# Sums over the partitions in a two-layer trunk: one fp32 matmul with ones against two fp32r matmuls on a split

## The chip, the core and the metric

The kernel runs on one core of a Trainium2 chip. The core has TensorE (PE in the profile, its weight loads PEld), VectorE (DVE), ScalarE (ACT), GpSimd (POOL) and SyncE (SP, which here issues the DMAs). Each engine takes its instructions in the order of its own queue and waits on semaphores for the others. The metric is device time in microseconds (us) of one execution, the median of several.

## The reference

The program is a decoder trunk of two layers on x of 1024 tokens by 1024 channels, in float32. In each layer the input is normalised, projected, and handed to four token mixers (latent attention "a", a gated convolution "b", a pooling "c", sliding-window attention "d"); their outputs are normalised per group, projected back and added; then comes a gated FFN of width 2816, normalised and added too. A last normalisation ends it. Every normalisation is this one:

```python
def rmsnorm(x, g):
    xf = x.astype(jnp.float32)
    y = xf * lax.rsqrt(jnp.mean(xf * xf, axis=-1, keepdims=True) + RMS_EPS)
    return (y * g.astype(jnp.float32)).astype(x.dtype)
...
for l in range(DEPTH):
    h = rmsnorm(x, attn_norm[l])
    proj = h @ w_in[l]
    ...
    q = (rmsnorm(c_q, q_norm_g) @ w_uq)
    kv = (rmsnorm(c_kv, kv_norm_g) @ w_ukv)
    ...
    gf = gf * lax.rsqrt(jnp.mean(gf * gf, axis=-1, keepdims=True) + RMS_EPS)   # per mixer
    x = x + mixed @ w_o[l]
    h2 = rmsnorm(x, ffn_norm[l])
    x = x + (jax.nn.silu(gate) * up) @ w_down[l]
return rmsnorm(x, final_norm)
```

## The kernel before

Activations lie with the channel on the partitions and the token along the row, so a tile is 128 channels by 512 tokens; the 1024 tokens are two halves t = 0 and 1. A sum over channels is therefore a sum over the partitions.

**Matrix products in three parts.** Products are made in the type fp32r. To keep more of the fp32 digits, each fp32 operand is split in two: `split` (L278 to L286) has ACT copy the tile into an fp32r tile `hi` (L280, or L283 with a gain) and DVE subtract that from the original into `lo` (L281 or L284). `mm3` (L264 to L276, its matmul is L269) then makes hi·hi, hi·lo and lo·hi into one PSUM bank. Nearly all of TensorE's instructions are of this line. In the FFN combinations of operands replace some of the products (lines named by B11 to T4), which does not touch the change.

**The norm.** `SumSq` holds the sum of squares of one normalisation, an accumulator `acc[t]` for each half. `add` squares a tile on ACT into a buffer of tag "tn" (L315; the first tile is squared straight into the accumulator, L310) and adds it on DVE (L321; the last addition also adds the epsilon, L317; L312 where there is one tile only). `rnorm` makes the reciprocal root: a matmul with a 128x128 tile of ones sums over the partitions and gives every partition the total (L327), ACT takes logarithm, exponential and square (L329, L330, L331), and one Newton step on DVE mends the digits (L332, L335), the last back into the accumulator. Callers then multiply by it (mostly through `mul_to`, L339).

`rnorm` is called 35 times: twice at the start (L364), in each layer twice for each of the four mixers' outputs (L608 for c, d and b, L1026 for a), twice for the key and value latents (L747), twice for the query latents (L788), twice ahead of the FFN (L1415), and at the end of a layer for the next norm (L1629 to L1641). In the last layer the second half is made in two pieces of 256 columns, so that gives three calls there.

**Buffers.** Most tiles live in 47 places of 128x1024 that `Slots` hands out. Scratch tiles come from `tmp`, with three tags: "te" has two buffers, "tn" three, "tp" three. "tn" is used by `add`, by `rnorm` (two a call), by the attention mixers' last steps (L575, L967) and by `snap` in the FFN. PSUM's eight banks have the tags "mm" (2), "s" (3), "t" (2) and "pv" (1); `rnorm` takes "t", before and after the FFN "pv", and for the last pieces "s". A buffer is used again once the instructions that read it have finished.

**Order.** The kernel is written for a tile framework: it places the waits, and when the program is built it lays each engine's instructions in an order that need not be that of the text. All DMAs of the main loop are issued by SP.

Of the kernel before, what the change touches and what calls it, by code (L numbers as in the profile page):

```python
# [11 lines left out]
F32 = mybir.dt.float32  # L12
F32R = mybir.dt.float32r
# [4 lines left out]
P = 128  # L18
# [3 lines left out]
HT = 512  # L22
# [88 lines left out]
def trunk_kernel(ctx: ExitStack, tc: tile.TileContext, ins, out):  # L111
    nc = tc.nc
    act, dve, pe, pool, sp = nc.scalar, nc.vector, nc.tensor, nc.gpsimd, nc.sync

    cpool = ctx.enter_context(tc.tile_pool(name="const", bufs=1))
    wpool = ctx.enter_context(tc.tile_pool(name="w", bufs=2))
    tpool = ctx.enter_context(tc.tile_pool(name="tmp", bufs=6))
# [7 lines left out]
    def rd(ap):  # L125
        return ap.bitcast(F32)
# [3 lines left out]
    pool.dma_start(par, ins["params"])  # L130
    cst = cpool.tile([P, CC_N], F32, name="cst")
    ident = cst[:, CC_ID : CC_ID + P]
    ones = cpool.tile([P, P], F32, name="ones")
    dve.memset(ones, 1.0)
    e_r = cpool.tile([P, P], F32R, name="e_r")
    nsink = cpool.tile([P, L * 4], F32, name="nsink")
    nffn = cpool.tile([P, L * NK], F32, name="nffn")
# [36 lines left out]
    def ps(tag):  # L174
        if tag in turns:
            turns[tag].rotate(-1)
            tag = turns[tag][-1]
        return psum.tile([P, HT], F32, name=f"ps_{tag}", tag=tag, bufs=PS_BUFS[tag])

    def tmp(tag="te"):  # L180
        return tpool.tile([P, HT], F32, name=tag, tag=tag, bufs={"te": 2, "tn": 3, "tp": 3}[tag])

    def small(n):
        return spool.tile([P, n], F32, name=f"sm{n}", tag=f"sm{n}", bufs=16 if n < 16 else 2)
# [93 lines left out]
    def split(hi, lo, f, gain=None):  # L278
        if gain is None:
            act.copy(hi, f)  # L280
            dve.tensor_tensor(out=lo, in0=f, in1=rd(hi), op=ALU.subtract)  # L281
        else:
            act.activation(hi, f, AF.Copy, scale=gain)  # L283
            dve.scalar_tensor_tensor(  # L284
                out=lo, in0=f, scalar=gain, in1=rd(hi), op0=ALU.mult, op1=ALU.subtract
            )  # L286
# [8 lines left out]
    class SumSq:  # L295
# [7 lines left out]
        def add(self, t, f, cols=whole):  # L303
            e = EPS * self.n / P
            m = self.done[t, cols.start] = self.done.get((t, cols.start), 0) + 1
            if self.acc[t] is None:
                self.acc[t] = F.half()
            a = F.ap(self.acc[t])[:, cols]
            if m == 1:
                act.activation(a, f, AF.Square)  # L310
                if self.n == P:
                    dve.tensor_scalar(out=a, in0=a, scalar1=e, scalar2=None, op0=ALU.add)  # L312
                return
            q = tmp("tn")[:, cols]
            act.activation(q, f, AF.Square)  # L315
            if m == self.n // P:
                dve.scalar_tensor_tensor(  # L317
                    out=a, in0=q, scalar=e, in1=a, op0=ALU.add, op1=ALU.add
                )
            else:  # L320
                dve.tensor_tensor(out=a, in0=a, in1=q, op=ALU.add)  # L321

        def rnorm(self, t, cols=whole, tag="t"):

            a, n = F.ap(self.acc[t])[:, cols], self.n
            p = ps(tag)[:, cols]
            pe.matmul(p, ones, a, start=True, stop=True)  # L327
            r0, q = tmp("tn")[:, cols], tmp("tn")[:, cols]
            act.activation(r0, p, AF.Ln, scale=1.0 / n)  # L329
            act.activation(r0, r0, AF.Exp, scale=-0.5)  # L330
            act.activation(q, r0, AF.Square)  # L331
            dve.scalar_tensor_tensor(  # L332
                out=q, in0=p, scalar=-0.5 / n, in1=q, op0=ALU.mult, op1=ALU.mult
            )
            dve.scalar_tensor_tensor(out=a, in0=q, scalar=1.5, in1=r0, op0=ALU.add, op1=ALU.mult)  # L335
            return self.acc[t]
# [41 lines left out]
    for l in range(L):  # L378
# [38 lines left out]
        def swa_q(m, pp):  # L417
            for t in range(2):
                f = tmp()
                dve.scalar_tensor_tensor(  # L420
                    out=f, in0=pp[t], scalar=0.125, in1=r_of(t), op0=ALU.mult, op1=ALU.mult
                )
                e, o = R.half(), R.half()
                qs[2 * m][t], qs[2 * m + 1][t] = e, o
                act.copy(R.ap(e)[hd], f[hd])
                act.copy(R.ap(o)[tl], f[tl])
                dve.tensor_tensor(
                    out=R.ap(e)[tl], in0=f[hd], in1=rd(R.ap(e)[hd]), op=ALU.subtract
                )
                dve.tensor_tensor(  # L430
                    out=R.ap(o)[hd], in0=f[tl], in1=rd(R.ap(o)[tl]), op=ALU.subtract
                )
# [40 lines left out]
        for t in range(2):  # L473
            f = tmp()
            mul_to(f, pv_[t], r_of(t))
            p = ps("t")
# [196 lines left out]
        for ct in range(2):  # L673
            pp = nextp
            u, a, b = F.pair(), F.pair(), F.pair()
# [36 lines left out]
            for t in range(2):  # L712
                h, lo = half_split(dst[:, t * HT : (t + 1) * HT])
                p = ps("t")
# [42 lines left out]
        for t in range(2):  # L757
            p = ps("mm")
            for k in range(NK):
                for n in range(2):  # L760
# [4 lines left out]
                        start=k == 0 and n == 0,  # L765
                        stop=k == NK - 1 and n == 1,
# [9 lines left out]
            p = ps("t")  # L776
# [804 lines left out]
        for n, (c, m) in enumerate(units):  # L1581
# [19 lines left out]
            p = banks["c" if c in (B21, N1, B22) else "a", m]  # L1601
# [169 lines left out]
```

## Time and profile before

| what | value |
|---|---|
| median of 3 runs | 2095.85 us (2094.59 to 2098.07) |
| span of the profiled execution | 2092.6 us |
| PE, DVE, ACT, POOL busy | 2057.8, 1493.1, 977.7, 539.8 us |
| matmuls of L327 | 70 (66 of 512 columns, 4 of 256) |
| granted TensorE clock | 0.998 of full speed |
| mean DMA rate | 138 GB/s |

The span runs from the first to the last instruction of the profiled execution; about 3 us lie around it in a run's time. In rows of groups the columns are line, engine, operation, output and inputs by name, shapes and count, then busy time and mean ns of one, then the idle time of the engine just before them with what ended it. In rows of the timeline they are start, duration, engine, line, operation, names, shapes and count, and in brackets the idle time before. Matmuls are pipelined: one that follows another shows a duration longer than the distance between their starts. In rows of windows the columns are the stretch, its length, and the busy time with the number of instructions of PE, PEld, DVE, ACT and POOL. In rows of the chain of waits they are start, duration and what the chain runs through.

### The profile page before, as it was taken

The page shows a single profiled execution, that of the slowest core. Times are in us where ns is not written, and L with a number is a line of the kernel's source. Part 1 is how long each engine was busy: PE and PEld are TensorE (multiplying, and loading weights), DVE is VectorE, ACT ScalarE, POOL GpSimd, SP SyncE. Part 2 cuts the span into 40 slices and gives each one's busy share as a digit, 9 for nine tenths or more (in the row PEclk, how much of TensorE's full clock was granted, in tenths as well). Part 3 has the DMA queues.
Part 4 walks back from the last instruction along what each step waited for, and adds up shares of the span by engine and source line. Part 5 has one row for each costly group of instructions (what it writes and reads, how often), then busy time and mean ns, then how long its engine had stood idle before and what let it go on. Part 6 is the DMA issues. An engine that isn't in the chain of part 4 may idle for free.

```text
span 2092.6 us, 26301 instructions
## 1 busy us (share of the span) xinstructions
PE 2057.8 (98%) x9442; PEld 1679.2 (80%) x9442; DVE 1493.1 (71%) x2407; ACT 977.7 (47%) x1706; POOL 539.8 (26%) x453
## 2 busy tenths in 40 slices
PE   8999999999999999999999999999999999999997
PEld 6777787888888888888888777877878888888887
DVE  6878977877666767566656889869666676675655
ACT  6446656653333334454433566657423333344442
POOL 0000000037676674200000000000467667541000
PEclk9999999999999999999999999999999999999999
DMA  4010122424444446886401102232354444378752
GB/s 178 33 51 26 68 87 73 161 72 169 172 156 151 166 161 201 290 289 220 147 28 51 46 13 92 68 117 100 112 180 161 143 174 156 126 259 312 260 178 88
DMA packets 148819, 289.76 MB, mean 138 GB/s; under 512 B 12608, under 2 KB 72000, under 8 KB 148688
## 3 DMA queue, kind: packets, MB, share of 16 engines
q1 hardware_dynamic: 148656, 288.03, 39.8%
q8 instruction: 74, 1.21, 0.2%
q14 instruction: 57, 0.47, 0.1%
q0 software_dynamic: 32, 0.04, 0.0%
HBM read 204.66 MB, written 83.36 MB: 138 GB/s over the span
## 4 chain that ended last, share of the span: by engine, by line
PE 92%; DVE 4%; ACT 2%; DMA 1%; issue 1%; POOL 0%; DVEq 0%; ACTq 0%; SPq 0%; POOLq 0%
PE ps_mm L269 35%; PE ps_s L269 28%; PE ps_t L269 12%; PE ps_pv L269 8%; PE ps_pv L953 2%; PE ps_t L941 1%; PE ps_t L327 1%; PE ps_s L887 1%; PE ps_pv L563 1%; PE ps_s L888 1%; PE ps_t L551 1%; PE ps_s L889 1%; PE ps_s L502 0%; DMA u<-in_w_o 0%; DVE u L281 0%
## 5 line engine op out<-in xcount | busy, mean ns | idle before, releaser
L269 PE MATMUL ps_mm<-u,u 128*128 128x512 f32 (+1 forms) x3376 | 825.2, 391 | 10.6 <-ACT u L283 6.9
L269 PEld LDWEIGHTS ps_mm<-u,u 128*128 128x128 f32 x3376 | 616.8, 189 | 132.9 <-ACT u L283 6.9
L269 PE MATMUL ps_s<-u,u 128*128 128x512 f32 x2672 | 630.8, 390 | 3.5 <-ACT tn L1167 3.5
L269 PEld LDWEIGHTS ps_s<-u,u 128*128 128x128 f32 x2672 | 501.5, 188 | 110.4 <-ACT tn L1167 4.3
L281 DVE TENSOR_TENSOR u<-u,u 128x1024 fp32r<-128x1024 f32 (+2 forms) x368 | 423.6, 1167 | 175.5 <-ACT u L280 155.3
L280 ACT CAST u<-u 128x1024 fp32r<-128x1024 f32 (+2 forms) x368 | 321.4, 897 | 485.1 <-PE ps_mm L269 182.3
L269 PE MATMUL ps_t<-u,u 128*128 128x512 f32 (+1 forms) x1212 | 274.5, 379 | 0.0
L269 PEld LDWEIGHTS ps_t<-u,u 128*128 128x128 f32 x1212 | 219.1, 188 | 44.1 <-issue 1.4
L950 POOL MEMSET u<- 128x128 f32 x32 | 6.4, 225 | 870.5 <-PE ps_mm L269 653.5
L158 POOL TENSOR_TENSOR u<-u 128x256 f32<-128x256 f32 x176 | 187.0, 1063 | 92.6 <-DMA u<-in_w_dn 62.7
L1303 POOL TENSOR_TENSOR tp<-tp,u 128x512 f32<-128x512 f32 x88 | 127.0, 1444 | 291.2 <-ACT tp L1302 290.9
L269 PE MATMUL ps_pv<-u,u 128*128 128x512 f32 x696 | 164.9, 389 | 0.0
L269 PEld LDWEIGHTS ps_pv<-u,u 128*128 128x128 f32 x696 | 130.7, 188 | 27.1
L1302 ACT ACTIVATE tp<-tp 128x512 f32<-128x512 f32 x88 | 55.5, 632 | 123.0 <-DVE tp L339 122.1
L280 ACT CAST u<-ps_t 128x512 fp32r<-128x512 f32 (+4 forms) x136 | 66.3, 505 | 67.4 <-PE ps_t L941 42.8
L281 DVE TENSOR_TENSOR u<-ps_t,u 128x512 fp32r<-128x512 f32 (+4 forms) x136 | 77.5, 582 | 25.7 <-ACT u L280 24.8
L283 ACT ACTIVATE u<-u,par 128x512 fp32r<-128x512 f32 x100 | 69.4, 715 | 51.2 <-DVE u L1090 16.5
L1123 POOL TENSOR_TENSOR u<-u,u 128x512 f32<-128x512 f32 x38 | 65.6, 1727 | 85.5 <-PE ps_s L269 44.5
L284 DVE SCALAR_TENSOR_TENSOR u<-u,par,u 128x512 fp32r<-128x512 f32 x100 | 72.8, 745 | 9.4 <-ACT u L283 9.1
L1515 DVE TENSOR_TENSOR tp<-ps_mm,tn 128x512 f32<-128x512 f32 x38 | 26.3, 692 | 68.7 <-PE ps_mm L269 68.7
L213 DVE TENSOR_TENSOR u<-u,u 128x1024 fp32r<-128x1024 f32 (+1 forms) x46 | 51.7, 1128 | 29.0 <-PE ps_t L269 10.0
L1296 DVE SCALAR_TENSOR_TENSOR u<-te,tp 128x512 f32<-128x512 f32 x38 | 44.9, 1182 | 36.8 <-POOL tp L1303 36.8
(188 smaller groups left out, 2248.7 us busy)
## 6 DMA issues: line engine op xcount, KB each, us to landing
u<-in_w_gu SPq DMA_DIRECT2D x88, 512.0 KB, 4.0
ad<-u SPq DMA_DIRECT2D x154, 256.0 KB, 2.2
u<-ad SPq DMA_DIRECT2D x70, 512.0 KB, 5.4
u<-in_w_dn SPq DMA_DIRECT2D x68, 512.0 KB, 3.8
qd<-u SPq DMA_DIRECT2D x44, 512.0 KB, 2.9
u<-qd SPq DMA_DIRECT2D x32, 512.0 KB, 5.2
u<-in_w_in SPq DMA_DIRECT2D x30, 512.0 KB, 3.5
u<-in_xT SPq DMA_DIRECT2D x32, 256.0 KB, 4.5
```

The lines of the kernel that those rows point to most:

```text
L158: pool.tensor_tensor(out=o, in0=o, in1=u, op=ALU.add)
L213: dve.tensor_tensor(out=lo[:, :n], in0=raw[:, :n], in1=rd(hi[:, :n]), op=ALU.subtract)
L269: pe.matmul(o, w, r, start=start and k == 0 and i == 0, stop=stop and k == n - 1 and i == 2, skip_group_check=again,)
L280: act.copy(hi, f)
L281: dve.tensor_tensor(out=lo, in0=f, in1=rd(hi), op=ALU.subtract)
L283: act.activation(hi, f, AF.Copy, scale=gain)
L284: dve.scalar_tensor_tensor(out=lo, in0=f, scalar=gain, in1=rd(hi), op0=ALU.mult, op1=ALU.subtract)
L953: pe.matmul(py[:, c0:], v_of(j, h), R.ap(s)[:, c0:], start=j == 0 and n == 0, stop=j == nj - 1 and n == 1,)
L1123: pool.tensor_tensor(out=F.ap(q + 1), in0=a21, in1=a22, op=ALU.add)
L1296: dve.scalar_tensor_tensor(out=o, in0=a, scalar=-1.0, in1=b, op0=ALU.mult, op1=ALU.mult)
L1302: last_silu = act.activation(g, g, AF.Silu)
L1303: pool.tensor_tensor(out=g, in0=g, in1=r, op=ALU.mult)
```

## The change

`rnorm` splits the accumulator into two fp32r tiles of tag "tn", with `split` as the products do, and makes two matmuls with ones, one for each part, into the same bank. The tile of ones is declared fp32r, and `tmp` takes a type. The rest of `rnorm` stays, so a call takes four buffers of "tn" where it took two, and issues one copy on ACT and one subtraction on DVE more.

```diff
-    ones = cpool.tile([P, P], F32, name="ones")
-    dve.memset(ones, 1.0)
+    ones = cpool.tile([P, P], F32R, name="ones")
+    dve.memset(ones.bitcast(F32), 1.0)
...
-    def tmp(tag="te"):
-        return tpool.tile([P, HT], F32, name=tag, tag=tag, bufs={"te": 2, "tn": 3, "tp": 3}[tag])
+    def tmp(tag="te", dt=F32):
+        return tpool.tile([P, HT], dt, name=tag, tag=tag, bufs={"te": 2, "tn": 3, "tp": 3}[tag])
...
             a, n = F.ap(self.acc[t])[:, cols], self.n
             p = ps(tag)[:, cols]
-            pe.matmul(p, ones, a, start=True, stop=True)
+            ah, al = tmp("tn", F32R)[:, cols], tmp("tn", F32R)[:, cols]
+            split(ah, al, a)
+            pe.matmul(p, ones, ah, start=True, stop=False)
+            pe.matmul(p, ones, al, start=False, stop=True)
             r0, q = tmp("tn")[:, cols], tmp("tn")[:, cols]
             act.activation(r0, p, AF.Ln, scale=1.0 / n)
```

## The prediction

> **What bounds the kernel now.** I read the page first: its head, the busy shares and the engine shares of the chain that ended last.
>
> ```profile
> span 2092.6 us, 26301 instructions
> PE 2057.8 (98%) x9442; PEld 1679.2 (80%) x9442; DVE 1493.1 (71%) x2407; ACT 977.7 (47%) x1706; POOL 539.8 (26%) x453
> PE 92%; DVE 4%; ACT 2%; DMA 1%; issue 1%; POOL 0%; DVEq 0%; ACTq 0%; SPq 0%; POOLq 0%
> ```
>
> TensorE sets the end for 92% of the span. Work taken off it there shortens the kernel; the 6% of the chain on DVE and ACT are where added steps of those two lengthen it. The question is on which part each `rnorm` lies. Next the view of line L327, the matmul that is replaced.
>
> ```profile
> L327 PE MATMUL ps_t<-u,ones x52: 590/592/697, 31.8 to 1408.9; 128*128 128x512 f32 x52
> L327 PE MATMUL ps_pv<-u,ones x14: 590/592/697, 415.9 to 2052.1; 128*128 128x512 f32 x14
> L327 PE MATMUL ps_s<-u,ones x4: 379/431/483, 2066.0 to 2082.9; 128*128 128x256 f32 x4
>   DVE u L317: 10.0, 12
> ```
>
> Seventy records make 35 calls: one fp32 matmul runs as two instructions. 33 calls are 512 columns wide, two 256. The last row says that TensorE sat idle before this line 12 times, 10.0 us in all, for L317, the addition that completes the sum of squares; before the other 23 it did not wait for it. Then the windows by engine, over the stretch of each layer where the calls crowd (the last row is the first window for L327 alone: 18 of its matmuls, so 9 calls, and the second has as many), and the time behind the first one.
>
> ```profile
> 180.00:240.00 60.00, 57.84 (x248) 43.45 (x246) 58.00 (x105) 42.91 (x81) 0.34 (x2) 1.00 0.10 34
> 1212.00:1272.00 60.00, 57.87 (x247) 43.36 (x246) 58.04 (x106) 42.73 (x82) 0.35 (x2) 1.00 0.10 33
> 260.00:365.00 105.00, 102.90 (x525) 82.18 (x524) 82.14 (x213) 60.78 (x148) 2.81 (x14) 1.00 0.25 81
> 180.00:240.00 60.00, 9.16 (x18) 2.88 (x18) 1.00 0.10 34
> ```
>
> In these two stretches DVE (third pair of numbers) is busy 58.00 of 60 us, as full as TensorE (first pair, 57.84). Later it has room (82.14 of 105). Last the timeline and the chain, which are quoted where they are used.
>
> **Removed: the fp32 matmul.** The timeline of TensorE around the first call, and a run of fp32r matmuls before it:
>
> ```profile
> 26.61 5.38 PE L269 MATMUL ps_s<-u,u 128*128 128x512 f32 x23
> 31.59 0.40 PE L269 MATMUL ps_s<-u,u 128*128 128x512 f32 x1
> 31.83 0.59 PE L327 MATMUL ps_t<-u,ones 128*128 128x512 f32 x1
> 32.26 0.59 PE L327 MATMUL ps_t<-u,ones 128*128 128x512 f32 x1
> 32.29 0.80 PE L269 MATMUL ps_s<-u,u 128*128 128x512 f32 x1
> ```
>
> The second half starts 0.43 us after the first. The fp32r matmul behind shows 0.80 us and ends at 33.09, where one of the usual 0.40 (second row) would have begun at 32.69, another 0.43 on. So the call holds the array for about 0.86 us. In the run of 23 fp32r matmuls the pitch is (5.38 - 0.40) / 22 = 0.23 us; the two new matmuls are of that form and take 0.46. That is 0.40 us less in each wide call, and half, 0.20, in a narrow one: 33 x 0.40 + 2 x 0.20 = 13.6 us of TensorE. The number of weight loads stays. The Trainium skill, "FP8 and Floating Point Precision", section "TensorE Precision Notes", has true FP32 at four passes; with four passes of the 0.23 us pitch a call would hold 0.92 us and the change would free 33 x 0.46 + 2 x 0.23 = 15.6 us. The row, 0.86, decides here.
>
> **Added: the split.** No call of before has it. The nearest forms are the split of a 128x512 SBUF tile, and for the narrow calls that of a 128x256 one:
>
> ```profile
> L280 ACT CAST u<-te 128x512 fp32r<-128x512 f32 x20 | 12.3, 615 | 3.8 <-DVE te L339 3.7
> L281 DVE TENSOR_TENSOR u<-te,u 128x512 fp32r<-128x512 f32 x20 | 13.7, 685 | 0.1
> L280 ACT CAST u<-vraw 128x256 fp32r<-128x256 f32 x2 | 0.8, 404 | 0.0
> L281 DVE TENSOR_TENSOR u<-vraw,u 128x256 fp32r<-128x256 f32 x2 | 0.8, 408 | 0.0
> 182.41 1.28 DVE L339 TENSOR_TENSOR u<-u,u 128x512 f32<-128x512 f32 x2
> ```
>
> ACT gets 35 copies, 21 us on an engine at 47%. DVE gets 35 subtractions; one shows 0.685 us, but back to back they follow at 1.28 - 0.68 = 0.60 us (last row), so 20.8 us in all. They bring two waits: DVE's subtraction waits for the copy, and everything in DVE's queue behind it waits too (evacuations of PSUM banks among it); the second matmul waits for the subtraction, with TensorE's queue behind it. No DMA is added and SP and POOL get nothing.
>
> What this costs where nothing hides it, read from the chain of waits in the prologue and at the end:
>
> ```profile
> 43.86 0.70 DVE u L317
> 44.61 1.14 PE ps_t L327 x2
> 45.83 0.61 ACT tn L329
> ...
> 48.58 0.70 DVE u L335
> ...
> 2082.09 0.44 DVE u L317
> 2082.57 0.71 PE ps_s L327 x2
> 2083.36 0.39 ACT tn L329
> ```
>
> From the end of L317 to the start of Ln (L329) is 45.83 - 44.56 = 1.27 us now. With the split, and hand-overs of 0.05 to 0.1 as between these rows: 0.1, copy 0.615, 0.05, subtraction 0.685, 0.05, second matmul 0.40, 0.1 = 2.0; so +0.7 us for a wide call on the chain, the saving on TensorE already inside. In the narrow one 0.84 now, and 0.1 + 0.40 + 0.05 + 0.41 + 0.05 + 0.28 + 0.1 = 1.39 then: +0.55. (0.28 is my estimate for a 256-column matmul, 0.40 less half a pitch.)
>
> Three calls stand alone on the chain so: these two, and one at the entry of the second layer's FFN, where TensorE waits for the addition:
>
> ```profile
> 1435.59 1.10 PE L327 MATMUL ps_pv<-u,ones 128*128 128x512 f32 x2 [0.94 <-DVE u L317]
> ```
>
> Together 0.7 + 0.7 + 0.55 = +1.9 us.
>
> **The crowded stretch** is the term I had to choose. The chain enters it through DVE, runs through TensorE, and near its end TensorE waits twice, for ACT and for DVE:
>
> ```profile
> 180.69 0.61 DVE u L317
> 181.43 1.96 PE ps_t L327 x4
> 183.39 2.75 PE ps_mm L761 x12
> ...
> 229.84 1.18 PE ps_s L269 x5
> ```
>
> ```profile
> 232.67 0.50 PE L887 MATMUL ps_s<-u,u 128*128 128x512 f32 x1 [1.04 <-ACT u L280]
> 239.21 1.13 PE L327 MATMUL ps_t<-u,ones 128*128 128x512 f32 x2 [0.92 <-DVE u L317]
> ```
>
> Nine calls give DVE 9 x 0.60 = 5.4 us of new work there, and it has 60 - 58.00 = 2.0 us idle. If DVE sets the pace, the stretch grows by 3.4 us when all its idle time can be used and by 5.4 when none can; TensorE's saving, 9 x 0.40 = 3.6, then only makes its waits longer. If TensorE sets the pace and DVE's backlog is work that nobody needs yet, the stretch shrinks by 3.6. So its growth x lies between -3.6 and +5.4 by these rows. I take the middle of the upper case, +4.4: the stretch ends, at 231 and 239 us, with TensorE waiting for DVE and ACT. It comes twice: +8.8.
>
> **The other calls.** 35 less 18 less 3 are 14, one of them narrow: 13 x 0.40 + 0.20 = 5.4 us saved. They lie where TensorE has other matmuls to run while the split is made and DVE is below 80% (260 to 365 us above). That cover exists because the order on an engine is not that of the text: a weight load of a much later step is issued before the first call.
>
> ```profile
> 27.57 0.77 SPq L209 DMA_DIRECT2D vraw<-in_w_uq  x1
> ```
>
> Without that cover each of the 14 would cost +0.7 instead of -0.4.
>
> **Sum:** 8.8 + 1.9 - 5.4 = +5.3 us on the profiled execution, whose span of 2092.6 is 3.25 below the median 2095.85. I add it to the median: 2101.1 us.
>
> **Rivals.** In all of them the time is 2095.85 + 2x + 1.9 - 5.4, and x decides; it breaks even at x = 1.75.
>
> (a) TensorE keeps the pace, x = -3.6, 2085.2 us: faster. For it: between the rows at 183.39 and 229.84 the chain runs through TensorE alone, and DVE can put off work whose results are needed late. Against it: the two waits above. It counts as faster from x below -0.35. If the three lone calls were covered too, the whole 13.6 would arrive: 2082.3. The Trainium skill, "Perfetto Trace Analysis", section "Identifying the Most-Contended Engine", says to improve the engine with the highest occupancy first, which is TensorE's 98% here; its next section adds that this engine may change between regimes, and the windows show just that.
>
> (b) DVE puts off part of the backlog, x between -0.35 and 3.85, about 2096: no change that could be measured.
>
> (c) Buffers. Tag "tn" has three; a call took two and now takes four, and the additions and snapshots use the tag too. It is tight already:
>
> ```profile
> 186.79 0.68 DVE L335 SCALAR_TENSOR_TENSOR u<-tn 128x512 f32<-128x512 f32 x1
> 187.57 0.63 ACT L331 ACTIVATE tn<-tn 128x512 f32<-128x512 f32 x1
> 207.68 0.68 DVE L335 SCALAR_TENSOR_TENSOR u<-tn 128x512 f32<-128x512 f32 x1
> ```
>
> L331 of one call, which takes a tn buffer, starts only when L335 of the call before has released its own (186.79 + 0.68 = 187.47). From the end of L317 (180.69 + 0.61 = 181.30) the first call takes 6.2 us to that point; alone, in the prologue, a call takes 48.58 + 0.70 - 44.56 = 4.7. If the calls can no longer overlap, the first five (they feed keys and queries) need 5 x (6.2 + 0.7) = 34.5 us; now the last of them ends with the third row, at 208.36, after 27.1. Then x is 7.4 and the time 2095.85 + 14.8 - 3.5 = 2107.1. It decides once the pieces of a later call hold two buffers while an earlier one needs its last.
>
> **Chances.** Less than about 0.2%, 4.2 us, can't be told from no change. Forecast (x over 3.85, DVE) 0.33; buffers 0.15; so slower 0.48. Rival (b) 0.25 same. Rival (a) 0.27 faster. The range runs from almost the full gain, 2083, past the buffers' 2107 to 2113 (the 14 covered calls half uncovered, 7 x 1.1 us, on top of the forecast's 2101 give 2109 too); some 0.15 is left outside it for an order of instructions that turns out quite differently. The forecast's own range is 2100 to 2104 (x from 3.85 to 5.4).
>
> **What would show it.** Right: in the windows of the two stretches DVE at 59 of 60 or more, the last L327 of the stretch later by 3 us or more after the first, and the waits near 232 and 239 us longer, while the other 14 calls start with no wait for L280 or L281. TensorE busy down by some 13 us and its idle time up by more. Rival (a): the same distance shorter, DVE's new work found after 240. Rival (c): Square or the copies waiting for a release of tn by DVE or PE. Wrong at the root: if the two new matmuls follow at more than 0.23 us each, or the copy and the subtraction cost clearly other than 0.62 and 0.60.

## The result and the profile after

The changed kernel takes 2122.43 us (median of 4 runs, 2120.34 to 2124.83) against 2095.68 for the kernel before: a ratio of 1.0131, 95% interval [1.0116, 1.0145], so 26.7 us slower. It is above the range of the forecast. The profiled execution has a span of 2123.1 us, 30.5 longer than the one of before. It is the slowest of the four runs, and differences between the two traces come out some 4 us larger than that of the medians.

The page of the changed kernel, head and busy shares:

```profile
span 2123.1 us, 26375 instructions
PE 2066.3 (97%) x9442; PEld 1685.6 (79%) x9442; DVE 1516.7 (71%) x2442; ACT 995.8 (47%) x1741; POOL 538.6 (25%) x453
```

DVE and ACT have 35 instructions more, as they should. TensorE, which was to lose 13 us of busy time, shows 8.5 more; the last section gives a part of the reason. Below the changed kernel's lines are L328 (the split), L329 and L330 (the two matmuls), L332 (Ln); L317 and the lines above it are those of before. In its timeline, the first call of all and two calls of the first crowded stretch show the parts of the change as they run. (The prediction counted nine calls in a stretch, those in its window of 60 us. A tenth stands just ahead of the window, at 176.26 and 1207.86 us in the kernel before. "First call" here is the first of the nine, the same one in every kernel.)

```profile
32.50 0.40 PE L329 MATMUL ps_t<-tn,ones 128*128 128x512 f32 x1
32.74 0.39 PE L330 MATMUL ps_t<-tn,ones 128*128 128x512 f32 x1
32.97 3.36 PE L269 MATMUL ps_s<-u,u 128*128 128x512 f32 x14
...
183.94 0.39 PE L329 MATMUL ps_t<-tn,ones 128*128 128x512 f32 x1
...
186.26 0.39 PE L330 MATMUL ps_t<-tn,ones 128*128 128x512 f32 x1
...
189.18 0.50 PE L329 MATMUL ps_t<-tn,ones 128*128 128x512 f32 x1
```

The starts lie 0.24 and 0.23 us apart: a call holds the array for 0.47 us, as worked out. But in the stretch the first call's second matmul comes 2.3 us after its first, with other work between, and the second call 5.2 us after the first. In the kernel before both calls ran in one group of four matmuls, at 181.43.

Where the time lies is read from the last call of each crowded stretch in the changed kernel's timeline (the first and the third row below; the second is the first call of the second layer's stretch), and, in a second fence, from the first and last call of the second layer's stretch in the kernel before:

```profile
255.65 0.50 PE L329 MATMUL ps_t<-tn,ones 128*128 128x512 f32 x1
...
1232.25 0.40 PE L329 MATMUL ps_t<-tn,ones 128*128 128x512 f32 x1
...
1301.22 0.50 PE L329 MATMUL ps_t<-tn,ones 128*128 128x512 f32 x1
```

```profile
1213.04 0.67 PE L327 MATMUL ps_t<-u,ones 128*128 128x512 f32 x1 [0.20 <-DVE u L317]
...
1270.76 1.12 PE L327 MATMUL ps_t<-u,ones 128*128 128x512 f32 x2 [0.92 <-DVE u L317]
```

From the first call of a stretch to its last it was 239.21 - 181.43 = 57.78 us in the first layer and 57.72 in the second; now it is 71.71 and 68.97. These two growths, 13.9 and 11.3, are 25.2 of the 30.5 us of span. Now the windows by engine for the changed kernel:

```profile
180.00:240.00 60.00, 52.26 (x193) 38.94 (x193) 50.35 (x83) 39.13 (x69) 0.34 (x2) 0.86 0.05 18
```

DVE was to be full here, 59 of 60. It is busy 50.35, less than before (58.00). Nothing is full: TensorE fell from 57.84 to 52.26, and its granted clock in this stretch to 0.86. The 60 us also hold less of the work than before: 193 of TensorE's matmuls, where there were 248. So the engines wait for each other. What TensorE waited for from 176 to 256 us, the view of waits (total, times, longest), before and then after:

```profile
PE ps_t L327 <- DVE u L317: 1.1, 2, 0.9
PE ps_s L887 <- ACT u L280: 1.0, 1, 1.0
```

```profile
PE ps_t L329 <- ACT tn L280: 4.4, 2, 4.0
PE ps_mm L269 <- DVE u L823: 1.8, 1, 1.8
PE ps_t L781 <- ACT u L280: 1.1, 1, 1.1
PE ps_t L330 <- DVE tn L281: 1.1, 1, 1.1
PE ps_s L890 <- ACT u L280: 1.0, 1, 1.0
PE ps_s L269 <- DVE u L284: 0.5, 1, 0.5
```

2.1 us of waits have become 9.9 in these rows. The wait for the new copy (first row) is the largest, but 3.4 us are new waits for operands that the change doesn't touch (L823, L280 ahead of L781, L284).

### The profile page after: what moved, and what is told of

It is laid out like the page before. It is cut to its first block, busy times and chain, and to the rows that moved or that the text cites. A ratio compares the mean times of both kernels' runs of the same rounds, so it can differ in the third digit from the quotient of the medians.

```text
span 2123.1 us, 26375 instructions
## 1 busy us (share of the span) xinstructions
PE 2066.3 (97%) x9442; PEld 1685.6 (79%) x9442; DVE 1516.7 (71%) x2442; ACT 995.8 (47%) x1741; POOL 538.6 (25%) x453
## 4 chain that ended last, share of the span: by engine, by line
PE 88%; DVE 5%; ACT 3%; DMA 2%; issue 1%; POOL 0%; DVEq 0%; ACTq 0%; SPq 0%; POOLq 0%
PE ps_mm L269 33%; PE ps_s L269 27%; PE ps_t L269 12%; PE ps_pv L269 7%; PE ps_pv L956 2%; PE ps_t L944 1%; PE ps_s L890 1%; ACT u L280 1%; PE ps_pv L566 1%; PE ps_s L892 1%; PE ps_s L891 1%; PE ps_t L554 1%; PE ps_mm L764 1%; DMA u<-in_w_o 1%; DMA u<-in_w_gu 1%
## 5 line engine op out<-in xcount | busy, mean ns | idle before, releaser
L269 PE MATMUL ps_mm<-u,u 128*128 128x512 f32 (+1 forms) x3376 | 834.0, 393 | 11.8 <-ACT u L283 7.1
L280 ACT CAST u<-u 128x1024 fp32r<-128x1024 f32 (+2 forms) x368 | 321.0, 897 | 479.9 <-PE ps_mm L269 179.0
L280 ACT CAST u<-ps_t 128x512 fp32r<-128x512 f32 (+4 forms) x136 | 66.7, 504 | 69.5 <-PE ps_t L944 39.5
L281 DVE TENSOR_TENSOR u<-ps_t,u 128x512 fp32r<-128x512 f32 (+4 forms) x136 | 78.2, 583 | 25.1 <-ACT u L280 23.9
L284 DVE SCALAR_TENSOR_TENSOR u<-u,par,u 128x512 fp32r<-128x512 f32 x100 | 72.1, 747 | 12.1 <-ACT u L283 11.7
```

The costliest lines, as they stand in the source:

```text
L269: pe.matmul(o, w, r, start=start and k == 0 and i == 0, stop=stop and k == n - 1 and i == 2, skip_group_check=again,)
L284: dve.scalar_tensor_tensor(out=lo, in0=f, scalar=gain, in1=rd(hi), op0=ALU.mult, op1=ALU.subtract)
```

## The experiments

Three theories stood against each other at first: work (the copy and the subtraction fill DVE and ACT), waiting (the matmul is held back by the 1.3 us of the split), and buffers (tag tn has three, a call needs four). A fourth came out of the runs.

**Where the loss sits: e6, e7.** The change is made only in the calls outside the two stretches (e6: mixer a, ahead of the FFN, and the 512-column calls at the ends of the layers, 11 in all), or only in the 20 calls of the stretches, ten in each layer (e7).

```diff
-        def rnorm(self, t, cols=whole, tag="t"):
+        def rnorm(self, t, cols=whole, tag="t", parts=False):
...
+            if parts:
+                ah, al = tmp("tn", F32R)[:, cols], tmp("tn", F32R)[:, cols]
+                split(ah, al, a)
+                pe.matmul(p, ones_r, ah, start=True, stop=False)
+                pe.matmul(p, ones_r, al, start=False, stop=True)
+            else:
+                pe.matmul(p, ones, a, start=True, stop=True)
```

> The change in 11 of the 35 calls only: mixer a, ahead of the FFN, and at the end of a layer, but for the two narrow ones; the calls of the two crowded stretches and of the prologue keep the fp32 matmul. If the loss is one of the stretches: no loss, TensorE's 11 x 0.40 = 4.4 us less, 2089 to 2096 us. If each call costs its share of the loss: 2101 to 2106.

> The change in the 20 calls of the two crowded stretches only (mixers b, c, d, key and value, query). If the loss is one of the stretches: the whole of it, 2118 to 2128 us. If each call costs its share: about 2111.

e6: 2094.95 us, ratio 0.9998 [0.9988, 1.0007]. e7: 2122.56 us, 1.0125 [1.011, 1.014]. The 20 calls cost all of it. The 11 others bring nothing that shows: by the prediction's own prices ten of them save 0.40 and the lone one costs 0.7, together -3.3 us, and the interval reaches to -2.5 only.

**Buffers: e2, e3, e12, e16, e1.** A fourth buffer for the change (e2), a fourth and one fewer for the kernel before (e12, e3), a fourth and a call that needs only three because the root is written into the sum (e16), and the parts in places of the slots instead of tn (e1).

```diff
-        return tpool.tile([P, HT], dt, name=tag, tag=tag, bufs={"te": 2, "tn": 3, "tp": 3}[tag])
+        return tpool.tile([P, HT], dt, name=tag, tag=tag, bufs={"te": 2, "tn": 4, "tp": 3}[tag])  # e2, e12, e16; e3 has "tn": 2
...
-            r0, q = tmp("tn")[:, cols], tmp("tn")[:, cols]
+            r0, q = a, tmp("tn")[:, cols]              # e16
...
-            ah, al = tmp("tn", F32R)[:, cols], tmp("tn", F32R)[:, cols]
+            h, lo = R.half(), R.half()                 # e1
+            ah, al = R.ap(h)[:, cols], R.ap(lo)[:, cols]
```

> The change with four buffers of tag tn and not three. Buffers: more than half of the loss goes, 2092 to 2108 us, since a call now fits whole but two still can't overlap fully. Work or latency: 2118 to 2125, no difference to the change.

> The kernel before, fp32 matmul and no split, with two buffers of tag tn and not three. Buffers: a loss like that of the change with no instruction added, 2105 to 2130 us. Work or latency: little, 2095 to 2102.

> The kernel before with four buffers of tag tn and not three. Buffers, if three were already short for two a call: 2085 to 2094 us. If three are enough before the change and only its four a call run short: 2094 to 2098.

> The change with four tn buffers and the reciprocal root written into the sum of squares, so that a call holds three of four buffers in place of four of three. Theory buffers (most of the loss is calls that wait for the buffers of the call before): 2105 us or less. Theory waiting (the split's 1.35 us ahead of each matmul): the time of the copy and maximum in place less the 13.6 us that TensorE saves, 2118.7 - 13.6 = 2105, if the saving arrives, and 2110 to 2118 if it doesn't.

> The change, but the two parts of the split lie in two half places of the slots and not in buffers of tag tn, so a call takes two of tn as before the change; instructions and their number are those of the change. Buffers (calls in a row can't overlap because each needs four of three buffers): the loss of 26.7 us goes, and what is left is TensorE's saving less the lone calls, 2085 to 2098 us; the distance from the third to the last call of the stretch (68 to 78 us in the changed kernel) comes back to about 63. Work (DVE and ACT have 35 instructions more each): as the change, 2115 to 2125. Latency (each call's sum is ready 1.4 us later): as the change, 2115 to 2125.

| run | us | ratio, 95% |
|---|---|---|
| e2 change, tn 4 | 2117.66 | 1.0106 [1.0091, 1.0121] |
| e3 before, tn 2 | 2111.56 | 1.0071 [1.0056, 1.0086] |
| e12 before, tn 4 | 2096.20 | 1.0 [0.9991, 1.001] |
| e16 change, tn 4, three needed | 2120.10 | 1.0114 [1.0099, 1.0129] |
| e1 change, parts in places | 2111.96 | 1.008 [1.0063, 1.0097] |

The kernel before has just enough buffers (e3, e12). For the change, 20.6 us of the loss of 26.7 are left with a fourth buffer (e2), and 23.9 in e16, where a call needs only three of the four; 2120.10 is above every range given for e16. In e1, whose parts take no buffer of tn at all, 14.9 us are left. That is more than a fourth buffer gives, but the places are a second change there, and 2111.96 lies between the ranges of the theories. So buffers are not the main part; how large their part is, these runs leave open.

**Work or waiting: e4, e5, e13, e14.** The kernel before, with its fp32 matmul, and ahead of it: a copy and a maximum of the sum in place, which the matmul must wait for (e4); the split into places that nobody reads (e5); the same work into a tile that takes no place (e13); an addition of zero on GpSimd, which only delays (e14).

```diff
+            act.copy(a, a)                                             # e4
+            dve.tensor_tensor(out=a, in0=a, in1=a, op=ALU.max)
...
+            h, lo = R.half(), R.half()                                 # e5
+            split(R.ap(h)[:, cols], R.ap(lo)[:, cols], a)
...
+            act.copy(junk[:, cols], a)                                 # e13
+            dve.tensor_tensor(out=junk[:, cols], in0=a, in1=a, op=ALU.max)
...
+            pool.tensor_tensor(out=a, in0=a, in1=zero[:, cols], op=ALU.add)   # e14
             pe.matmul(p, ones, a, start=True, stop=True)
```

> The kernel before, with the fp32 matmul, where each call first copies the accumulator onto itself on ACT and then takes the maximum of it with itself on DVE: the work and the delay of the split (0.62 and 0.69 us, one behind the other), no buffer more and nothing saved on TensorE. Work or latency: most of the loss and TensorE's 13.6 us on top, 2115 to 2135 us. Buffers: 2097 to 2110.

> The kernel before with its fp32 matmul; each call also splits the accumulator into two half places of the slots, and nobody reads the parts: ACT's and DVE's work of the change, without the wait of TensorE on it and without buffers of tn. Work (DVE is full in the two stretches): a loss like that of e4_in_place, 2108 to 2120 us. Latency (the sum is ready 1.4 us later and everything behind waits): 2096 to 2103, with no half clock in the trace.

> The kernel before with a copy on ACT and a maximum on DVE of the sum of squares ahead of each matmul, written to a tile that nobody reads and that takes no place of the slots: the work of the split alone, 35 instructions on each engine, while the fp32 matmul waits for neither. Theory work (DVE and ACT have no room in the two crowded stretches, as the prediction had it): at least +4.4 us for each stretch, so 2105 us or more. Theory waiting (the loss comes from the matmul being held back, not from the busy time): within 4 us of the kernel before, 2096 to 2100.

> The kernel before with one addition of a zero tile to the sum of squares on GpSimd ahead of each matmul: GpSimd's additions of 128x512 take 1.36 to 1.73 us in the kernel before, about the copy and the subtraction together (1.3 us), and GpSimd is idle three quarters of the time; ACT and DVE get no work, tag tn is left alone. Theory waiting: most of the 21.7 us that the copy and the maximum in place cost, so 2108 to 2120. Theory work: only the three lone calls pay, 3 x 1.5 = 4.5 us, so about 2100.

| run | us | ratio, 95% |
|---|---|---|
| e4 work and delay | 2118.71 | 1.0108 [1.0093, 1.0124] |
| e5 work, in places | 2108.43 | 1.0059 [1.0042, 1.0076] |
| e13 work, in a tile of its own | 2111.25 | 1.0072 [1.0057, 1.0087] |
| e14 delay, on GpSimd | 2119.97 | 1.0111 [1.0096, 1.0126] |

Both theories hold, and that is too much: the work alone costs 15.0 us, the delay alone 23.8, and both together no more than the delay, 21.7. If these were costs of work and waiting in one fixed course of events they would add up better than that. (e13 is not quite work alone: the last step of `rnorm` writes into the sum, and so waits until the copy and the maximum have read it.)

**TensorE's saving: e8 to e11, e15.** Only the high part goes through one fp32r matmul (e8). Then the last addition of the sum writes it rounded to fp32r, into a place (e9: the 20 calls of the stretches; e10: 31 calls; e11: 11 calls outside; in e10 and e11 the last 256 tokens' norm is made of an incomplete sum). e15 keeps the sums in fp32r tiles from the start, in all calls.

```diff
+            h = R.half()                                               # e8
+            ah = R.ap(h)[:, cols]
+            act.copy(ah, a)
+            pe.matmul(p, ones, ah, start=True, stop=True)
...
-                    out=a, in0=q, scalar=e, in1=a, op0=ALU.add, op1=ALU.add   # e9 to e11
+                    out=o, in0=q, scalar=e, in1=a, op0=ALU.add, op1=ALU.add
...
-                self.acc[t] = F.half()                                 # e15
+                self.acc[t] = R.half()
```

> As e1_slots with the high part alone: one fp32r matmul on a rounded copy, no subtraction and no second matmul, the copy in a half place; the low part of the sums is left out. DVE gets nothing more and the sum is ready 0.7 us later and not 1.4. Work on DVE: the loss of e1_slots turns into the gain of TensorE's 35 x 0.63 = 22 us, 2074 to 2084. Latency: half of it stays, 2088 to 2100.

> The kernel before; in the 20 calls of the crowded stretches the last addition (L317, or L312) writes its sum in fp32r into a half place, and one fp32r matmul takes the place of the fp32 one; no instruction, no wait and no buffer of tn more, the sum is rounded and its low part left out. TensorE gets 20 x 0.63 = 12.6 us less and nothing is added elsewhere. If TensorE set the pace in the stretches (then the loss of the change is all added work): 2083 to 2087 us. If DVE, ACT and the waits of the calls on one another set it: little of it, 2090 to 2097.

> The same in 31 of 35 calls, all but the four ahead of the FFN: 29 x 0.63 + 2 x 0.3 = 18.9 us of TensorE saved with nothing added. If TensorE set the pace everywhere: 2075 to 2080. If the stretches are set by the other engines: 2083 to 2092. If removing time from TensorE's calls brings nothing anywhere, since idle time takes its place: 2093 to 2098.

> The same in the 11 calls outside the stretches alone (prologue, mixer a, end of a layer): 9 x 0.63 + 2 x 0.3 = 6.3 us of TensorE. If what TensorE saves outside the stretches counts: 2088 to 2091. If idle time takes its place there too: 2094 to 2098.

> The kernel before with the sums of squares kept in fp32r tiles (rounded at every addition; the low part is left out) and one fp32r matmul in place of the fp32 one: no instruction, place or buffer more, 33 x 0.63 + 2 x 0.3 = 21.4 us of TensorE less (one matmul of 0.23 us for 0.86). If TensorE's time is what the calls cost, 2075 us. If the calls in the crowded stretches are timed by the chain over ACT and DVE, only the calls outside gain, as in the earlier run of eleven of them (2.2 us): 2085 to 2095.

| run | us | ratio, 95% |
|---|---|---|
| e8 high part | 2098.57 | 1.0016 [1.0007, 1.0026] |
| e9 rounded, stretches | 2108.81 | 1.0058 [1.0041, 1.0075] |
| e10 rounded, 31 calls | 2101.37 | 1.0025 [1.0016, 1.0035] |
| e11 rounded, outside | 2093.76 | 0.9987 [0.9978, 0.9997] |
| e15 rounded, all calls | 2099.14 | 1.0012 [1.0002, 1.0021] |

In the stretches, less work for TensorE makes a longer time (e9, where the place that it takes is a second change); only outside them some of it arrives, 2.3 us of 9 x 0.63 + 2 x 0.3 = 6.3 in e11. The times of e9, e10 and e15 lie outside every range that was given for them. e15 adds no instruction and takes work from TensorE, and the kernel got no faster but a little slower. Its view of TensorE's waits from 176 to 256 us has waits that the kernel before didn't have (its lines are 3 further than those of before):

```profile
PE ps_t L781 <- ACT u L283: 3.2, 1, 3.2
PE ps_s L272 <- ACT u L286: 3.0, 2, 2.0
```

No theory of work, waiting or buffers gives this. Its sums lie in other places than before (the slots keep fp32 and fp32r apart), which can delay other tiles, so it isn't TensorE's saving alone. But TensorE's matmuls also come in another sequence than before in the stretch, in this kernel as in the change, e4, e13, e14 and e16. In the kernels that are not slower, e6, e11 and e12, the sequence in the stretches, the matmuls with ones left out, is that of before (in e12 but for 8 places). That is the fourth theory: the order of instructions on the engines, which the framework lays out anew for each program, costs the time.

**The order: e17, e18.** e17 is the kernel before, with the fp32 matmuls and without the split, but every instruction, DMA issues among them, stands on its engine in the order that it has in the changed kernel. e18 is e4 with everything but the copy and the maximum held in the order of before. Both are made with edges that only order.

```diff
+        _seq = np.frombuffer(_dz(_b85(ORDER)), "<u2")
+        _info = _mybir.DependencyInfo(_mybir.DependencyClass.NoSync, _mybir.DependencyReason.DATA)
+        _prev = {}
+        for _k in _seq.tolist():
+            _i = _base[_k]
...
+                _p = _prev.get(_j.engine)
+                if _p is not None:
+                    tc.add_manual_dep(_j, _p.name, _info, reason="order")
+                _prev[_j.engine] = _j
```

> The kernel before, with the same instructions, buffers and fp32 matmuls, but on every engine in the order in which the changed kernel has them (the split and the second matmul have no counterpart and are skipped). Theory order (the order that is laid out anew for the changed program costs the time, not the split itself): most of the loss, 2110 us or more. Theory waiting (the split's 1.3 us ahead of each matmul and the tn buffers that it holds): the order alone costs little, 2096 to 2102 us.

> The kernel with the copy and the maximum in place (e4, 2118.7 us), but with all other instructions on every engine held in the order of the kernel before. Theory order: what is left is the wait in the three lone calls, 3 x 1.35 us, so 2098 to 2102 us. Theory waiting: the 1.35 us ahead of each of the nine matmuls of a stretch still stand, so 2110 us or more.

e17: 2122.11 us, ratio 1.0136 [1.0119, 1.0152]. The old work in the new order takes the time of the change, 2122.43. Its busy shares:

```profile
PE 2066.4 (98%) x9442; PEld 1682.6 (79%) x9442; DVE 1494.8 (71%) x2407; ACT 976.8 (46%) x1706; POOL 536.2 (25%) x453
```

DVE and ACT have as many instructions as before (2407 and 1706). In the trace all of these stand in the sequence of the changed kernel with the split left out, and so do TensorE's matmuls but for those with ones, of which the second half follows the first at once. Its timeline at the first two calls of the stretch, around the two waits of 2.07 us, and at the last call (its lines, too, are 3 further):

```profile
184.03 1.02 PE L330 MATMUL ps_t<-u,ones 128*128 128x512 f32 x2
184.49 1.26 PE L764 MATMUL ps_mm<-u,u 128*128 128x512 f32 x3
185.59 4.02 PE L272 MATMUL ps_mm<-u,u 128*128 128x512 f32 x17
189.45 1.02 PE L330 MATMUL ps_t<-u,ones 128*128 128x512 f32 x2
...
219.28 1.02 PE L330 MATMUL ps_t<-u,ones 128*128 128x512 f32 x2
219.74 0.74 PE L891 MATMUL ps_s<-u,u 128*128 128x384 f32 x1
220.31 0.33 PE L892 MATMUL ps_s<-u,u 128*128 128x384 f32 x1
220.49 1.09 PE L272 MATMUL ps_mm<-u,u 128*128 128x512 f32 x4
223.64 1.13 PE L330 MATMUL ps_t<-u,ones 128*128 128x512 f32 x2 [2.07 <-DVE u L320]
226.83 5.52 PE L272 MATMUL ps_mm<-u,u 128*128 128x512 f32 x13 [2.07 <-DVE u L216]
...
252.68 1.02 PE L330 MATMUL ps_t<-u,ones 128*128 128x512 f32 x2
```

The second call stands 20 matmuls behind the first, though in this kernel no split and no buffer asks for that. From the first call to the last it is 252.68 - 184.03 = 68.65 us, 10.9 more than before, against 13.9 in the change. In the second layer it is 10.9 more too (1228.69 to 1297.27 us). The two waits of 2.07 us show how an order costs time. On DVE, in the same kernel:

```profile
222.30 0.69 DVE L335 SCALAR_TENSOR_TENSOR tn<-ps_t,tn 128x512 f32<-128x512 f32 x1 [0.37 <-ACT tn L334]
222.91 0.68 DVE L320 SCALAR_TENSOR_TENSOR u<-tn,u 128x512 f32<-128x512 f32 x1
...
225.56 1.23 DVE L216 TENSOR_TENSOR u<-u,u 128x1024 fp32r<-128x1024 f32 x1
```

The addition that completes the next sum (L320) stands behind the Newton step of the call before (L335), which waits for ACT; TensorE waits for that addition. Behind them stands the low part of a weight tile (L216), and TensorE's next matmul waits for that. The kernel before has the same two calls, and the same two steps of DVE one behind the other:

```profile
207.91 1.10 PE L327 MATMUL ps_t<-u,ones 128*128 128x512 f32 x2
208.44 4.47 PE L269 MATMUL ps_mm<-u,u 128*128 128x512 f32 x17
212.75 1.02 PE L327 MATMUL ps_t<-u,ones 128*128 128x512 f32 x2
```

```profile
211.28 0.68 DVE L332 SCALAR_TENSOR_TENSOR tn<-ps_t,tn 128x512 f32<-128x512 f32 x1
211.88 0.68 DVE L317 SCALAR_TENSOR_TENSOR u<-tn,u 128x512 f32<-128x512 f32 x1
```

TensorE does not wait there. 17 matmuls stand between its two calls and last until the sum is ready; in e17 six stand there (the rows from 219.74), and the rest of the time is idle. So the wait was there to be covered all along, and what differs is where TensorE's other matmuls stand.

e18: 2161.37 us, 1.0312 [1.0296, 1.0327]. The order theory had 2098 to 2102 for it, and fell on that point. Here TensorE, DVE and ACT have the sequence of before throughout, the copy and the maximum apart. With it kept, those two cost 65.8 us, where the same work in an order laid out for it (e4) costs 21.7. TensorE's waits for the matmuls of the calls, over the whole kernel (L331 is the maximum in place):

```profile
PE ps_t L333 <- DVE u L331: 30.8, 15, 2.8
PE ps_pv L333 <- DVE u L331: 19.7, 3, 14.3
```

And in the kernel before:

```profile
PE ps_t L327 <- DVE u L317: 2.2, 4, 0.9
```

So the waiting is real, at up to 2.8 us a call in ps_t. One wait of 14.3 us, ahead of the second layer's FFN, depends on where the maximum came to stand in DVE's queue, since the copy and the maximum were left free (the copy ends at 1484.27 us, the maximum starts at 1496.12); it is no price of the delay as such. With that wait taken off, some 50 of the 65.8 us are left.

Together: the old order leaves no room for a copy and a maximum ahead of the matmul (e18). The order that the framework lays out for the changed kernel costs 26.6 us without any split in it (e17), and the changed kernel, with the split, costs 26.7. One comparison is missing: no run holds the kernel before in its own order, so that the edges by themselves cost nothing is not shown. That e17's waits are for data (L320, L216) speaks for it.

## Why the prediction was wrong

The direction was right, the size was not: +26.7 us for a forecast of +5.3, and 9 us over the top of the range. The mechanism was not right either: the forecast was slower because DVE would be full, and it isn't, so the direction is in part luck. The rival that was left outside the range, an order of instructions that turns out quite differently, is what came.

**Removed: the fp32 matmul.** 0.46 us a call was forecast, 0.47 measured. That part of TensorE's 13.6 us would arrive is not borne out: nothing of it shows in the stretches, and outside them e6 leaves room for 2.5 us at the most.

**Added: the split.** A copy on the chain takes 0.63 us (second row below), as in the row chosen. For a lone call +0.7 us was forecast (+0.55 narrow). The chain of the changed kernel, at the second call and at the last:

```profile
44.30 0.70 DVE u L317
...
45.08 0.63 ACT tn L280
...
45.75 0.50 PE ps_t L329
46.25 0.70 PE ps_t L269 x3
46.95 0.25 PE ps_t L330
...
47.28 0.61 ACT tn L332
...
2112.06 0.44 DVE u L317
...
2113.92 0.39 ACT tn L332
```

From the end of L317 to the start of Ln it is 47.28 - 45.00 = 2.28 us, 1.0 more than before: three other matmuls stand between the two halves. In the narrow call it is 1.42, 0.58 more. These two terms were right within 0.3 us. The third lone call, ahead of the second layer's FFN, waits for nothing in the changed kernel: its matmuls start at 1488.65 and 1488.88 us, where 1435.59 was the place before, behind matmuls that now stand ahead of it. For it +0.7 was wrong; its place in TensorE's order is another, in e17 too (1485.46).

**The crowded stretch** is the step that failed, x = +4.4 in each layer; 13.9 and 11.3 were measured between the first and the last call. The step bounded x by DVE's room, 9 x 0.60 us of new work against 2.0 us of idle time, and so took the order of the engines' instructions for given. The changed program gets another order, and that order alone costs 10.9 us in each stretch (e17). DVE at 58 of 60 did not give the price: in the changed kernel DVE is busy 50.35 of 60, and the stretch is longer. Whether DVE set the pace in the old order, no run isolates. What the runs suggest, without showing it, is that the 58 marks an order in which TensorE, DVE and ACT fit closely, and that a shift undoes it: of the eighteen kernels of the experiments, the fourteen that put something into the calls of the stretches, took something out of them or took a buffer away are all slower than before, by 0.12% to 3.1%.

**The other calls.** -5.4 us for 14 of them was too good. For the 11 of e6, -3.3 by the same prices is outside what was measured. Two of the 14 are the tenth calls of the stretches, which e6 leaves as they were.

**Rival (c), buffers,** put its finger on something that is there, calls that no longer overlap (5.2 us from the first to the second), but three buffers are not the main reason: with four the change is still 1.0106, and with the parts in places 1.008. Its own sign, squares or copies of tn that wait for a release of tn by DVE or PE, is not in the trace of the first stretch: the copies there wait for L317, their data.

**What would show it.** The last call of the stretch later by more than 3 us, and no wait for the split in the other 14 calls: right. DVE at 59 or more, TensorE's busy time 13 us lower: wrong. The two waits near the end of the stretch longer: wrong as well. The one ahead of L887 was 1.0 us and is 1.0 (L890 above), the one ahead of the last call is gone, and the new long ones are 4.0 us ahead of the call at 226.94 and 1.8 us for L823.

What stays open: which of the change's constraints moves the order most. The delay alone (e14) cost 23.8 us, the work alone (e13) 15.0, one buffer fewer (e3) 14.5; each of these kernels has an order of its own, so they are not costs that can be added. And that e17 and the change come out equal leaves open whether, in the new order, the split and TensorE's saving cost nothing or cancel. They lose their time in part differently: the change has more of it at half clock, as the last section shows.

## What to carry to other kernels

Where a framework lays out the order of the instructions, an edit changes two things, the instructions and the order of all others near them; a sum made from the old trace prices only the first. In this kernel, in stretches where several engines are nearly full at once, the second was the larger, and a loss even for edits that add no work (e9, e15). It can be measured by itself: run the old instructions in the new order, and the new ones in the old. The old ones held in the old order belong to it, to see that holding an order costs nothing.

## What the hardware showed

TensorE's granted clock fell to half five times inside the changed kernel, three of them in the stretches. In the profiled execution of the kernel before it fell only at 2084 us, when the last matmul was done. Views of the changed kernel: two windows of 3.41 us just ahead of the first two falls and the sum over the five pieces at half clock (in the windows the last three columns are granted clock, DMA share and GB/s), then its timeline in the first piece:

```profile
197.73:201.14 3.41, 1.75 (x7) 0.71 (x5) 2.85 (x5) 3.29 (x6) 0.00 (x0) 1.00 0.32 120
221.62:225.03 3.41, 1.34 (x5) 0.56 (x3) 2.92 (x11) 1.97 (x4) 0.00 (x0) 1.00 0.00 0
...
sum 30.72, PE 25.25 PEld 17.90 DVE 23.88 ACT 14.31 POOL 3.67; mean PE 5.05 PEld 3.58 DVE 4.78 ACT 2.86 POOL 0.73
```

```profile
202.96 4.52 PE L269 MATMUL ps_mm<-u,u 128*128 128x512 f32 x10
207.28 0.63 PE L330 MATMUL ps_t<-tn,ones 128*128 128x512 f32 x1
```

Ten matmuls take (207.28 - 202.96) / 10 = 0.43 us each instead of 0.23. TensorE is busy for 25.25 us at half clock, and at full clock the same work would take 25.25 x 0.23 / 0.43 = 13.5; so about 12 us of TensorE's time, by this estimate, come from the clock. That is a part of the reason why its busy time rose although the calls got shorter. In e17 it is busy 9.66 us at half clock, in two pieces, which gives some 4.5 us. So a wait can be paid for twice. How much of the 12 us reaches the end of the kernel, no run shows.

The Trainium skill, "TensorE: Matmul & The Clock Gate", section "HAM oscillation — how this bites in real kernels", gives the rule that TensorE should have no idle gaps of more than about 3.4 us. Only one of the five falls fits that length, the one at 1272.92 us, 3.4 us into a wait of 4.0. At 225.03 the clock fell when a wait of the same length had lasted 2.1 us, and at 201.14 the waits ahead were 0.52 and 1.14 us. In the 3.41 us ahead of the five falls TensorE was busy 1.75, 1.34, 1.72, 0.00 and 1.54 us, about half the time or less.
